# Retention outputs copied from their banks and normalised by ScalarE, row scaling on VectorE, background blocks loaded one call ahead

## The chip, the core and the metric

The kernel runs on one core of a Trainium2 chip. The core's engines are named here as the profile names them: PE (TensorE, matmuls; PEld is its weight load), DVE (VectorE), ACT (ScalarE), POOL (GpSimd) and SP (SyncE, which issues most DMAs). The metric is the device time of one execution in microseconds (us). Before the change the median of 3 runs is 3018.64 us (3012.9 to 3021.43).

## What is computed

The reference is a trunk of two layers on 1024 rows of width 1024, batch 1, all in float32. The mixer of layer 0 is a gated delta net, that of layer 1 a retention; each layer ends with a convolutional feed-forward, and each half of a layer with a layer norm. Scale, shift and gate vectors come from a conditioning vector by a product with `ada_w`, six vectors per layer.

```
e = silu(c @ cond_w + cond_b)
for i in range(2):
    mod = e @ ada_w[i] + ada_b[i]
    sh1, sc1, g1, sh2, sc2, g2 = split(mod, 6)
    y = mixers[i](x * (1 + sc1) + sh1)
    x = layer_norm(ALPHA * x + (1 + g1) * y, ln_g[i, 0], ln_b[i, 0])
    y = conv_ffn(x * (1 + sc2) + sh2, ...)
    x = layer_norm(ALPHA * x + (1 + g2) * y, ln_g[i, 1], ln_b[i, 1])
```

Retention has 4 heads (keys of 256, values of 512) and works in 8 chunks of 128 rows. A chunk's output is a masked score product plus the running state times the scaled queries; each row of it, 512 wide, is then standardised and gated:

```
o = intra + inter                       # per head and chunk: 128 x 512
o = (o - mean(o)) * rsqrt(var(o) + 1e-6)
o = o * silu(gate)
y = o @ w_out
```

## The kernel before

**Order of the work.** The stages follow each other: the delta net (to about 620 us in the profile), its output projection with layer norm, the first feed-forward (Strassen-like products `strassen`, then the down projection `proj_gen`), retention's projections (again `strassen`, 1440 to 1785), retention's chunks (1785 to 2180), its output projection, and the second feed-forward. Large products run as three float32r matmuls of a high and a low part; `split` (L88) makes the parts, the high one on ACT (L89), the low one on DVE (L90).

The kernel is written in a language whose scheduler puts instructions on the engines. It takes them in the order of the program, skips what isn't ready in its own time model, gives a tile a buffer of its tag (`BUFS`, L43: a tag and its number of buffers) when one is free, and sets the semaphores. On the chip each engine then runs its list in order, and so does each DMA queue. For the delta net and retention's chunks a planner of the kernel itself (`run`, L649) fixes the order on PE: generators yield a delay in planned microseconds, a matmul adds its price to the planned clock (`pm`, L637, 0.216 each), a transpose 0.109 (`ptr`), and the generator of the lowest priority number that is due goes next. What a generator yields after it hands work to the other engines is the time that the plan grants them; for retention these are in `RL` (L1799).

**Background work.** `bg` is a list of small units that don't belong to the stage in which they run. `bg_step` (L119) takes the first and runs it; it is called after a weight block in the delta net's filler, in `ret_v` (L1672), twice in each item `wino` of `strassen` (L1233, L1238), and in the projections. There are two kinds of unit.
- `bg_ada` (L201): a modulation vector, 8 units each. A unit loads a block of `ada_w`, 128 x 2 x 512 (`mvw`, L210), on SP, and DVE multiplies it by two values of `e` per row and adds (L214, L216). The tile's tag is `wr`, in `strassen` `lane` (`bg_tag`).
- `bg_gain` (L370): 16 units that multiply a block of 128 x 512 of the second-layer input by `ln_g` and add `ln_b` on POOL (L381, L382), and store it. The tile's tag is `lane`. Its only call is L1817, ahead of retention's chunks; its units run in the first 16 calls from `ret_v`.

**The tag `wr`.** It has two buffers of 4 KB per partition. They hold the raw weights of `load_w` (L100), both halves `wa` and `wb` of an item in `wino` (L1211), the blocks of `bg_ada`, some blocks in `proj_gen`, and at the start four transposed input blocks (`hold`, L532). `hold` puts two more into the tag `xT`, which nothing else uses.

**Retention's chunks.** `core(h)` (L1704) goes through the chunks of head h. Per chunk it makes the products of the keys with the values into two `sc` banks and the new state from them on DVE (L1728, L1730), calls `ret_front` (L1680) for the next chunk (scores and scaled keys, `kz` on ACT and DVE, `sThl`, and `qx` on POOL, L1701), and then the output `po` in an `sc` bank. There are two `sc` banks, and a chunk takes three in turn, so a bank in which `po` stands is wanted again by the next chunk's second key product. `ret_back` (L1748) works on the output: statistics from the bank on DVE (L1750, L1752), plus 1e-6 (L1753), to the power -0.5 on POOL (L1754, a 128 x 1 instruction), and the normalisation from the bank into `on` on DVE (L1756). It yields `RL["b"]`; then PE transposes `on` (L1763), DVE multiplies by the gate (L1765), and the blocks go to memory, some after sums on POOL (L1787). `on` shares the tag `t2` (3 buffers) with `kz`. Between the chunks, `ret_fill` (L1802) gives PE the value projections (`ret_v`) and the first two products of the output projection.

Of the kernel before, what the change touches and what calls it, by code (L numbers as in the profile page):

```python
# [12 lines left out]
ALU = mybir.AluOpType  # L13
AX = mybir.AxisListType

P = 128
# [17 lines left out]
def trunk_kernel(ctx: ExitStack, tc, A):  # L34
# [9 lines left out]
            "wr": 2, "wh": 2, "wl": 2, "t2": 3, "sm": 14, "sm2": 6, "st": 8, "s8": 6, "S": 4, "qx": 3, "fs": 1, "xT": 2}  # L44
# [74 lines left out]
    def bg_step(tile=mm_tile):  # L119
        bg_ps[0] = tile  # L120
        if bg:
            bg.pop(0)()
# [78 lines left out]
    def bg_ada(i, j, kind):  # L201
        box = {}

        def unit(nh, kp):
# [3 lines left out]
            wr = tl(bg_tag[0], [P, 2, HALF], name="mvw")  # L208
            c0 = j * D + nh * HALF
            sp.dma_start(wr, A["ada_w"][i, kp * 256:(kp + 1) * 256, c0:c0 + HALF].rearrange("(a p) n -> p a n", p=P))  # L210
# [30 lines left out]
        for nh in range(2):  # L241
            for kp in range(KT // 2):
                bg.append(lambda nh=nh, kp=kp: unit(nh, kp))
# [126 lines left out]
    def bg_gain(n, src, dst):  # L370
        gb = []

        def unit(c, r):
# [7 lines left out]
            pool.tensor_tensor(x, x, gb[0], ALU.mult)  # L381
            pool.tensor_tensor(x, x, gb[1], ALU.add)  # L382
# [149 lines left out]
    def hold(half, fs):  # L532
        for f in fs:
# [4 lines left out]
            else:  # L538
                t = tl("auh" if half else "xT", [P, HALF], name="xT")
# [614 lines left out]
    def strassen(hT0, xts, scale, shift, items, tags=("hTb", "hTb", "qkv", "qkv", "aux"), direct=False):  # L1154
        B = {"11": hT0[:4], "21": hT0[4:]}
# [592 lines left out]
    def ret_back(h, n, po):  # L1748
        st = tl("st", [P, 2, 6], name="rst")
        dve.bn_stats(st[:, 0], po)  # L1750
        mv = tl("s8", [P, 4], name="mv")
        dve.bn_aggr(mv[:, 0:2], st[:, 0])  # L1752
        dve.tensor_scalar(mv[:, 2:3], mv[:, 1:2], 1e-6, None, ALU.add)  # L1753
        pool.tensor_tensor(mv[:, 3:4], mv[:, 2:3], mhalf[:, 0:1], ALU.pow)  # L1754
        on = tl("t2", [P, HALF], name="on")
        dve.tensor_scalar(on, po, mv[:, 0:1], mv[:, 3:4], ALU.subtract, ALU.mult)  # L1756
# [42 lines left out]
    RL = {"v": 2.57, "q": 5.9, "f": 3.35, "p": 0.55, "c": 2.75, "b": 3.21, "o": 4.42}  # L1799
# [17 lines left out]
    bg_gain(1, xs[1], xg[0])  # L1817
# [106 lines left out]
```

## Time and profile before

| | us |
|---|---|
| median of 3 runs | 3018.64 |
| the profiled execution | 3028.18 |
| its span in the trace | 3026.4 |
| mean granted PE clock | 0.974 |
| PE, DVE, ACT, POOL busy | 2846.3, 2248.8, 1316.6, 672.8 |

How to read the profile's lines: a group or an instruction is given by its line in the kernel (L90 is a helper's, so the tile names tell what it works on), its engine, and out<-in by the tiles' names. A group's line ends with busy time, mean ns of one, and the idle time of its engine just before, with what ended it. In a list of waits, "A <- B: 7.5, 4, 4.1" says that A's engine stood idle for B, 7.5 us in 4 places, the longest 4.1. In a list by time the first number is the start in us, the second the duration, and brackets hold the idle time ahead and its releaser; SPq and ACTq are the queues from which DMAs are issued. In a list of an instruction's line, three numbers after the count are its shortest, median and longest ns. `sc`, `acc` and `mm` are PSUM banks.

### The profile page before, as it was taken

Reading aid. Unit: us, or ns where it says so; the run is one execution under the profiler, and the core shown is the slowest. Engines: PE = TensorE matmul, PEld = TensorE weight load, DVE = VectorE, ACT = ScalarE, POOL = GpSimd, SP = SyncE. Lnnn points to the kernel's source line nnn. Section 1 sums busy time; section 2 is a strip of 40 time slices with the busy share of each in tenths; the row PEclk is TensorE's granted clock in tenths of the full one; section 3 lists DMA queues with packets and bytes.
Section 4 is the critical chain, followed back from the end, with each engine's and each line's share of the span. In section 5 each row is a group of like instructions: output and inputs, shape, how many; then the busy total and the mean of one; then the engine's idle time right before and its main releaser. Section 6 shows DMA issues by size and latency. Waiting matters only on the chain.

```text
span 3026.4 us, 38855 instructions
## 1 busy us (share of the span) xinstructions
PE 2846.3 (94%) x13638; PEld 2316.4 (77%) x13638; DVE 2248.8 (74%) x3805; ACT 1316.6 (44%) x2409; POOL 672.8 (22%) x629
## 2 busy tenths in 40 slices
PE   8889998999999999998999999999998899999997
PEld 7768877887778888786777787767776688888785
DVE  5785786545778888998688645666788787778988
ACT  4655555434544444445433342221343544445442
POOL 0410311034011111630023302532200011113704
PEclk9999998999999999999999999999999999999998
DMA  7222222344344444864322444656663343335662
GB/s 274 87 70 74 97 82 64 116 163 137 105 153 156 154 153 158 322 201 154 129 91 101 173 155 143 212 175 181 210 224 123 108 139 105 105 104 202 250 196 108
DMA packets 243027, 450.22 MB, mean 149 GB/s; under 512 B 22928, under 2 KB 76432, under 8 KB 242832
## 3 DMA queue, kind: packets, MB, share of 16 engines
q1 hardware_dynamic: 211648, 400.02, 40.1%
q10 hardware_dynamic: 29760, 43.00, 3.9%
q0 software_dynamic: 1424, 4.72, 0.4%
q8 instruction: 107, 1.75, 0.2%
q14 instruction: 88, 0.72, 0.1%
HBM read 339.13 MB, written 108.53 MB: 148 GB/s over the span
## 4 chain that ended last, share of the span: by engine, by line
PE 34%; DVE 10%; DMA 6%; issue 3%; ACT 1%; POOL 1%; SPq 0%; POOLq 0%; DVEq 0%; ACTq 0%
PE acc L638 6%; PE acc L1160 5%; PE acc L110 3%; PE acc L111 3%; PE acc L112 3%; PE sc L1160 2%; PE sc L638 2%; PE acc L279 2%; PE acc L280 2%; PE acc L278 2%; DVE ab L90 1%; PE sc L110 1%; PE sc L112 1%; PE sc L111 1%; DVE bb L90 1%
## 5 line engine op out<-in xcount | busy, mean ns | idle before, releaser
L638 PE MATMUL acc<-hT,wh 128*128 128x512 f32 x960 | 304.4, 399 | 0.0
L1558 POOL TENSOR_TENSOR o<-o 128x512 f32<-128x512 f32 x88 | 118.8, 1360 | 726.7 <-DVE o L1551 653.5
L1160 PE MATMUL acc<-T,wb 128*128 128x512 f32 x840 | 208.8, 399 | 14.6 <-DVE wb L90 14.6
L279 PE MATMUL acc<-bb,ab 128*128 128x512 f32 x504 | 203.3, 403 | 18.6 <-DVE bb L90 18.5
L638 PEld LDWEIGHTS acc<-hT,wh 128*128 128x128 f32 x960 | 185.5, 193 | 34.9
L278 PE MATMUL acc<-bb,ab 128*128 128x512 f32 x504 | 191.7, 404 | 20.2 <-DVE ab L90 11.5
L638 PE MATMUL acc<-hT,wl 128*128 128x512 f32 x480 | 205.7, 429 | 0.2 <-ACT sg L1086 0.2
L1160 PEld LDWEIGHTS acc<-T,wb 128*128 128x128 f32 x840 | 160.3, 192 | 53.1 <-DVE wb L90 19.7
L280 PE MATMUL acc<-bb,ab 128*128 128x512 f32 x504 | 200.7, 399 | 0.0
L89 ACT ACTIVATE ab<-ar 128x512 fp32r<-128x512 f32 x210 | 129.7, 624 | 163.1 <-PE acc L280 84.0
L90 DVE TENSOR_TENSOR wb<-wr,wb 128x512 fp32r<-128x512 f32 x162 | 116.1, 719 | 102.3 <-ACT wb L89 102.3
L90 DVE TENSOR_TENSOR ab<-ar,ab 128x512 fp32r<-128x512 f32 x210 | 177.0, 850 | 13.8 <-ACT ab L89 13.5
L90 DVE TENSOR_TENSOR wl<-wr,wh 128x1024 fp32r<-128x1024 f32 x85 | 107.3, 1262 | 96.8 <-ACT wh L89 96.8
L90 DVE TENSOR_TENSOR wb<-mm,wb 128x512 fp32r<-128x512 f32 x216 | 144.7, 683 | 20.8 <-ACT wb L89 18.8
L89 ACT ACTIVATE wh<-wr 128x1024 fp32r<-128x1024 f32 x101 | 106.8, 1059 | 120.5 <-PE acc L638 48.3
L1217 ACT ACTIVATE pc<-acc 128x512 f32<-128x512 f32 x143 | 84.7, 593 | 166.2 <-PE acc L1160 95.3
L89 ACT ACTIVATE wb<-mm 128x512 fp32r<-128x512 f32 x216 | 122.3, 593 | 67.1 <-DVE mm L1206 66.2
L89 ACT ACTIVATE wb<-wr 128x512 fp32r<-128x512 f32 x162 | 98.6, 626 | 97.8 <-DMA wr<-in_ffn_up 50.7
L638 PE MATMUL acc<-wh,hT 128*128 128x512 f32 x384 | 136.5, 418 | 1.6 <-DVE vv L90 1.6
L457 DVE SCALAR_TENSOR_TENSOR qkv<-raw,vc,qkv 128x512 f32<-128x512 f32 x144 | 114.6, 800 | 30.4 <-ACT qkv L455 29.2
L1537 DVE SCALAR_TENSOR_TENSOR o<-g,vc,o 128x512 f32<-128x512 f32 (+2 forms) x176 | 134.7, 783 | 1.2 <-ACT o L1532 0.5
L278 PEld LDWEIGHTS acc<-bb,ab 128*128 128x128 f32 x504 | 96.1, 193 | 47.9 <-DVE ab L90 13.1
(634 smaller groups left out, 7774.6 us busy)
## 6 DMA issues: line engine op xcount, KB each, us to landing
wr<-in_ffn_up SPq DMA_DIRECT2D x96, 512.0 KB, 4.1
mvw<-in_ada_w SPq DMA_DIRECT2D x80, 512.0 KB, 4.3
ad<-o SPq DMA_DIRECT2D x154, 256.0 KB, 2.6
ar<-ad SPq DMA_DIRECT2D x154, 256.0 KB, 4.7
Br<-in_ffn_down SPq DMA_DIRECT2D x88, 256.0 KB, 3.7
wr<-in_ret_wv SPq DMA_DIRECT2D x32, 512.0 KB, 3.7
ar<-od SPq DMA_DIRECT2D x56, 256.0 KB, 5.4
xs<-xt ACTq DMA_DIRECT2D x24, 512.0 KB, 3.4
```

The costliest lines, as they stand in the source:

```text
L89: act.activation(dst_h, src, AF.Copy)
L90: eng.tensor_tensor(dst_l, src, dst_h, ALU.subtract)
L110: mm(acc, wl[:, k], hl[0], start=first, stop=False)
L111: mm(acc, wh[:, k], hl[1], start=False, stop=False)
L112: mm(acc, wh[:, k], hl[0], start=False, stop=last)
L278: mm(acc, a[1][:, sl], w[0], start=first, stop=False)
L279: mm(acc, a[0][:, sl], w[1], start=False, stop=False)
L280: mm(acc, a[0][:, sl], w[0], start=False, stop=last)
L638: pq(pe.matmul(out, lhsT, rhs, start=start, stop=stop), cost)
L1160: return pe.matmul(*a, skip_group_check=True, **kw)
L1537: dve.scalar_tensor_tensor(tv, gv[:, c0 - j:c1 - j], w[:, 2 - j:3 - j], tv, ALU.mult, ALU.add)
L1558: pool.tensor_tensor(o[d], o[x], o[y], op)
```

## The change

1. `bg_step` issues the load of the next unit, where that has one that can go ahead (`fetch`), before it runs the current unit. A unit is now a pair of its fetch and its work. `bg_flush` runs a unit whose load is out already, at the start and at the end of `strassen`, so that no loaded tile crosses the change of tag.
2. `wr` has 3 buffers instead of 2. The tag `xT` is gone; its two tiles are `cv` tiles now.
3. `bg_gain` takes its tiles from `wr`, and its multiplication and addition run on the engine given, DVE for its only call. The first block of each column half has no fetch ahead.
4. `ret_back`: ACT copies `po` from the bank to `on`; the statistics are taken from `on`; the factor and the shift (minus mean times factor) are made by small instructions, two on DVE and two on POOL; ACT normalises `on` in place with them. `RL["b"]` is 6.0 instead of 3.21.

```diff
-            "wr": 2, "wh": 2, "wl": 2, "t2": 3, ..., "fs": 1, "xT": 2}
+            "wr": 3, "wh": 2, "wl": 2, "t2": 3, ..., "fs": 1}
...
-    def bg_step(tile=mm_tile):
+    def bg_step(tile=mm_tile, ahead=True):
         bg_ps[0] = tile
         if bg:
-            bg.pop(0)()
+            unit = bg.pop(0)[1]
+            if ahead and bg and bg[0][0]:
+                bg[0][0]()
+                bg_ahead[0] = True
+            else:
+                bg_ahead[0] = False
+            unit()
+
+    bg_ahead = [False]
+
+    def bg_flush():
+        if bg_ahead[0]:
+            bg_step(ahead=False)
...
     def bg_ada(i, j, kind):
         box = {}
+        def fetch(nh, kp):
+            wr = box[nh, kp] = tl(bg_tag[0], [P, 2, HALF], name="mvw")
+            c0 = j * D + nh * HALF
+            sp.dma_start(wr, A["ada_w"][i, kp * 256:(kp + 1) * 256, c0:c0 + HALF].rearrange("(a p) n -> p a n", p=P))
+
         def unit(nh, kp):
...
-            wr = tl(bg_tag[0], [P, 2, HALF], name="mvw")
-            c0 = j * D + nh * HALF
-            sp.dma_start(wr, A["ada_w"][i, kp * 256:(kp + 1) * 256, c0:c0 + HALF].rearrange("(a p) n -> p a n", p=P))
+            if (nh, kp) not in box:
+                fetch(nh, kp)
+            wr = box.pop((nh, kp))
...
-                bg.append(lambda nh=nh, kp=kp: unit(nh, kp))
+                bg.append((lambda nh=nh, kp=kp: fetch(nh, kp), lambda nh=nh, kp=kp: unit(nh, kp)))
...
-    def bg_gain(n, src, dst):
-        gb = []
-
-        def unit(c, r):
+    def bg_gain(n, src, dst, eng=pool):
+        gb, box = [], {}
+
+        def fetch(c, r):
             if r == 0:
                 gb[:] = [tl("auh", [P, HALF], name="gb") for _ in range(2)]
                 for t, nm in zip(gb, ("ln_g", "ln_b")):
                     sp.dma_start(t, A[nm][n:n + 1, hs(c)].to_broadcast([P, HALF]))
-            x = tl("lane", [P, HALF], name="xg")
-            rs = slice(r * P, r * P + P)
-            sp.dma_start(x, src[rs, hs(c)])
-            pool.tensor_tensor(x, x, gb[0], ALU.mult)
-            pool.tensor_tensor(x, x, gb[1], ALU.add)
-            sp.dma_start(dst[rs, hs(c)], x)
+            x = box[c, r] = tl("wr", [P, HALF], name="xg")
+            sp.dma_start(x, src[r * P:r * P + P, hs(c)])
+
+        def unit(c, r):
+            if (c, r) not in box:
+                fetch(c, r)
+            x = box.pop((c, r))
+            eng.tensor_tensor(x, x, gb[0], ALU.mult)
+            eng.tensor_tensor(x, x, gb[1], ALU.add)
+            sp.dma_start(dst[r * P:r * P + P, hs(c)], x)
...
-                bg.append(lambda c=c, r=r: unit(c, r))
+                bg.append((r and (lambda c=c, r=r: fetch(c, r)), lambda c=c, r=r: unit(c, r)))
...
-                t = tl("auh" if half else "xT", [P, HALF], name="xT")
+                t = tl("auh", [P, HALF], name="xT") if half else tl("cv", [P, 516], name="xT")[:, 0:HALF]
...
     def strassen(hT0, xts, scale, shift, items, tags=("hTb", "hTb", "qkv", "qkv", "aux"), direct=False):
+        bg_flush()
...
+        bg_flush()
         bg_tag[0] = "wr"
         return B
...
     def ret_back(h, n, po):
         st = tl("st", [P, 2, 6], name="rst")
-        dve.bn_stats(st[:, 0], po)
+        on = tl("t2", [P, HALF], name="on")
+        act.activation(on, po, AF.Copy)
+        dve.bn_stats(st[:, 0], on)
         mv = tl("s8", [P, 4], name="mv")
         dve.bn_aggr(mv[:, 0:2], st[:, 0])
-        dve.tensor_scalar(mv[:, 2:3], mv[:, 1:2], 1e-6, None, ALU.add)
-        pool.tensor_tensor(mv[:, 3:4], mv[:, 2:3], mhalf[:, 0:1], ALU.pow)
-        on = tl("t2", [P, HALF], name="on")
-        dve.tensor_scalar(on, po, mv[:, 0:1], mv[:, 3:4], ALU.subtract, ALU.mult)
+        dve.tensor_scalar(mv[:, 1:2], mv[:, 1:2], 1e-6, None, ALU.add)
+        dve.tensor_scalar(mv[:, 2:3], mv[:, 0:1], -1.0, None, ALU.mult)
+        pool.tensor_tensor(mv[:, 3:4], mv[:, 1:2], mhalf[:, 0:1], ALU.pow)
+        pool.tensor_tensor(mv[:, 2:3], mv[:, 2:3], mv[:, 3:4], ALU.mult)
+        act.activation(on, on, AF.Identity, bias=mv[:, 2:3], scale=mv[:, 3:4])
         yield RL["b"]
...
-    RL = {"v": 2.57, "q": 5.9, "f": 3.35, "p": 0.55, "c": 2.75, "b": 3.21, "o": 4.42}
+    RL = {"v": 2.57, "q": 5.9, "f": 3.35, "p": 0.55, "c": 2.75, "b": 6.0, "o": 4.42}
...
-    bg_gain(1, xs[1], xg[0])
+    bg_gain(1, xs[1], xg[0], dve)
```

More of the change, by code (lines that the diff above doesn't have):

```diff
@@ L43, in trunk_kernel @@
     BUFS = {"hTa": 8, "hTb": 8, "qkv": 24, "aux": 4, "auh": 8, "lane": 4, "cv": 4, "ada": 1,
-            "wr": 2, "wh": 2, "wl": 2, "t2": 3, "sm": 14, "sm2": 6, "st": 8, "s8": 6, "S": 4, "qx": 3, "fs": 1, "xT": 2}
+            "wr": 3, "wh": 2, "wl": 2, "t2": 3, "sm": 14, "sm2": 6, "st": 8, "s8": 6, "S": 4, "qx": 3, "fs": 1}
     def tl(tag, shape, dt=F32, name=None):
```

## The prediction

> **What bounds the kernel now.** I read the page first (span and engines), then the busy times by stage, then who waits for whom on PE within two stages, then the instructions in order of time around the longest of those waits.
>
> ```profile
> span 3026.4 us, 38855 instructions
> PE 2846.3 (94%) x13638; PEld 2316.4 (77%) x13638; DVE 2248.8 (74%) x3805; ACT 1316.6 (44%) x2409; POOL 672.8 (22%) x629
> ```
>
> PE is busy 94% of the span, so all waits of PE together are worth 3026.4 - 2846.3 = 180 us. The change takes no matmul away. What it can win is part of these 180 us and the slow clock that follows idle time. The stages that the change reaches (stretch, its length, busy us and instructions of PE, weight load, DVE, ACT and POOL, then PE's clock, DMA share, GB/s):
>
> ```profile
> 0.00:620.00 620.00, 559.60 (x3648) 475.69 (x3649) 425.33 (x1016) 328.06 (x698) 105.74 (x169) 0.95 0.32 108
> 1440.00:1690.00 250.00, 238.90 (x1052) 193.81 (x1052) 193.36 (x269) 85.34 (x143) 58.64 (x39) 1.00 0.32 111
> 1785.00:2180.00 395.00, 372.24 (x1660) 287.95 (x1659) 242.98 (x430) 100.65 (x169) 123.96 (x168) 0.99 0.60 186
> 2180.00:2355.00 175.00, 158.59 (x678) 125.94 (x678) 139.57 (x232) 74.20 (x125) 10.58 (x13) 0.95 0.51 176
> 2355.00:2775.00 420.00, 411.15 (x1791) 336.61 (x1790) 319.05 (x483) 200.20 (x339) 55.58 (x41) 0.99 0.34 112
> ```
>
> In order: the delta net (60 us of idle PE), retention's Strassen projections (11), retention's chunks (23), retention's output projection (16), the second feed-forward's Strassen products (9). In the chunk stage PE waits for these:
>
>
> ```profile
> PE sc L638 <- DVE on L1756: 7.5, 4, 4.1
> PE mm L641 <- DVE on L1756: 5.1, 3, 2.5
> ```
>
> The first row is a matmul that wants the `sc` bank still held by a chunk's output, the second the transposes of that output; together 12.6 of the 23 us. The longest one, in order of time:
>
> ```profile
> 1869.37 0.70 DVE L1750 BATCH_NORM_STATS2 rst<-sc 128x6 f32<-128x512 f32 x1 [0.75 <-PE sc L638]
> 1870.96 1.29 POOL L381 TENSOR_TENSOR xg<-xg,gb 128x512 f32<-128x512 f32 x1 [8.78 <-DMA xg<-xs]
> 1872.21 1.84 POOL L1701 TENSOR_TENSOR qx<-qk,dx 128x128 f32<-128x128 f32 x2
> 1874.02 1.25 POOL L382 TENSOR_TENSOR xg<-xg,gb 128x512 f32<-128x512 f32 x1
> 1876.06 0.54 POOL L1754 TENSOR_TENSOR mv<-mv,mhalf 128x1 f32<-128x1 f32 x1
> 1876.63 0.81 DVE L1756 TENSOR_SCALAR on<-sc,mv 128x512 f32<-128x512 f32 x1 [3.31 <-POOL mv L1754]
> 1877.50 1.65 PE L638 MATMUL sc<-vv,kz 128*128 128x512 f32 x3 [4.05 <-DVE on L1756]
> ```
>
> The statistics were ready soon after 1870.1, but the tiny power instruction stood on POOL behind the row gains (L381, L382, loaded late) and `qx`, and the bank was freed only by L1756, 8 us after bn_stats began. Without that queue 0.70 + 0.18 + 0.15 + 0.54 + 0.81, about 2.4 us, would do.
>
> **The change part by part.** Prices of single instructions:
>
> ```profile
> L1756 DVE TENSOR_SCALAR on<-sc,mv 128x512 f32<-128x512 f32 x32 | 25.9, 809 | 32.0 <-POOL mv L1754 32.0
> L1752 DVE BATCH_NORM_AGGREGATE mv<-rst 128x2 f32<-128x6 f32 x32 | 5.7, 178 | 0.7
> L1753 DVE TENSOR_SCALAR mv<-mv 128x1 f32<-128x1 f32 x32 | 4.9, 154 | 1.1
> L1754 POOL TENSOR_TENSOR mv<-mv,mhalf 128x1 f32<-128x1 f32 x32 | 17.9, 561 | 83.6 <-DVE mv L1753 83.6
> L381 POOL TENSOR_TENSOR xg<-xg,gb 128x512 f32<-128x512 f32 x16 | 22.4, 1404 | 86.7 <-issue 49.5 <-DMA xg<-xs 37.2
> L90 DVE TENSOR_TENSOR wb<-wr,wb 128x512 fp32r<-128x512 f32 x162 | 116.1, 719 | 102.3 <-ACT wb L89 102.3
> L1217 ACT ACTIVATE pc<-sc x73: 574/597/602, 853.5 to 2786.9; 128x512 f32<-128x512 f32 x73
> L1374 ACT ACTIVATE xt<-xt,mv x8: 799/814/819, 2966.8 to 3020.0; 128x512 f32<-128x512 f32 x8
> ```
>
> *Loads of the engines.* DVE loses 32 x 0.809 = 25.9 and gains 32 x 0.154 = 4.9 for the sign and 32 x 0.719 = 23.0 for the gains: +2 us on 243 busy of 395 (a gain has two inputs in SBUF like the subtraction that it is priced as; that took 1.44 beside POOL in the row of 1573.33 below, which would make it +25). POOL loses 32 gains at 1.40 (44.9; L382 is priced as L381) and gets 32 multiplications, not shown and priced as the power at 0.561 (18.0): -27. ACT gets 32 x (0.597 + 0.814) = +45 on 101 of 395. None becomes full.
>
> *(a) Bank and chain.* The `sc` bank is freed by the copy, 0.6 us after the last matmul instead of 2.4 to 8. That takes the 7.5 us row away unless ACT is late. The output's own chain grows: 0.60 copy, 0.70 statistics (on SBUF now, priced as from the bank), 0.18, two times 0.15, two times 0.56, 0.81: 3.7 us against 2.4. The planner however places the transposes 6.00 instead of 3.21 after the last matmul. Slack goes from 0.8 to 2.3 us, and the gains leave POOL's queue. Of the 5.1 us of late transposes I expect half to stay. Sum 7.5 + 2.5 = **10 won**, between 0 and 12.6. Queued behind the waiting ACT instruction are `kz`, `sThl` and the weight splits; ACT idles before most `kz` (row in the rivals), which is their cover.
>
> *(b) Background loads one call ahead.* The same DMAs on SP, each issued one call earlier. In the chunk stage two waits of DVE for a modulation block stop PE:
>
> ```profile
> 2007.91 1.90 DVE L216 SCALAR_TENSOR_TENSOR ada<-mvw,e,ada 128x512 f32<-128x512 f32 x2 [6.43 <-DMA mvw<-in_ada_w]
> 2011.54 0.50 PE L638 MATMUL acc<-wl,22_12882 128*128 128x512 f32 x1 [2.20 <-DVE wl L90]
> 2016.60 0.75 DVE L216 SCALAR_TENSOR_TENSOR ada<-mvw,e,ada 128x512 f32<-128x512 f32 x1 [3.86 <-DMA mvw<-in_ada_w]
> 2019.80 0.96 PE L638 MATMUL sc<-vv,sThl 128*128 128x512 f32 x3 [2.76 <-DVE Sr L1728]
> ```
>
> 10.3 us of DVE's wait cost PE 5.0, about half. Loaded a call earlier both vanish: **4.5 won**, between 0 and 5. Against that, the first gain block of each column half isn't fetched ahead and now stops DVE, not POOL. POOL's waits for such loads were 37.2 us over 16 blocks (row of L381), 2.3 each; two of them, of which PE sees half: **2 lost**, between 0 and the 8.8 of the longest (row of 1870.96). A load that is called for earlier also stands earlier in SP's queue, and when its buffer isn't free, the gate loads, weights and stores behind it wait:
>
> ```profile
> L210 SPq EVENT_SEMAPHORE  x55: 17/28/8337, 59.2 to 2453.2; - x55
> ```
>
> SP has waited up to 8.3 us there, 0.03 in the median; I price it at nothing, because the third buffer is added at the same time. In the delta net:
>
> ```profile
> DVE ada L216 <- DMA mvw<-in_ada_w: 11.8, 10, 2.1
> PE mm L638 <- DVE DT L955: 19.8, 2, 11.0
> ```
>
> There DVE runs the triangular solve without a break up to the two long PE waits, so a microsecond of its waits is one of PE's. Only some of the ten lie in those stretches: **3 won**, between 0 and 11.8.
>
> *(c) Third `wr` buffer.* In the rotary items of the Strassen projections both halves of an item's weights are requested only after the last use of the previous ones:
>
> ```profile
> PE acc L1160 <- DVE wb L90: 4.7, 4, 1.7
> PE sc L1160 <- DVE wb L90: 3.2, 3, 1.3
> 1568.40 0.33 SPq L1212 DMA_DIRECT2D wr<-in_ret_wqk  x1
> 1571.82 0.69 DVE L1151 TENSOR_TENSOR pc<-sc,pc 128x512 f32<-128x512 f32 x1 [2.14 <-PE sc L1160]
> 1572.67 1.16 ACT L89 ACTIVATE wb<-wr 128x512 fp32r<-128x512 f32 x2 [3.02 <-DMA wr<-in_ret_wqk]
> 1573.33 2.88 DVE L90 TENSOR_TENSOR wb<-wr,wb 128x512 fp32r<-128x512 f32 x2 [0.82 <-ACT wb L89]
> ```
>
> ACT waits 3.02 us for the load and DVE stands idle 2.14 + 0.82 there; some 13 us later DVE is behind and PE waits up to 1.7. With a third buffer the first block is in before, and the 2.9 us of splits move into that idle time. Of 7.9 us I take **6 won**, between -3 (a new order of DVE's work) and 7.9. What the third buffer does in the feed-forward stages I leave at nothing: their loads lie beside matmuls that keep PE busy 411 of 420 us, and if the new order of DVE's work uncovers them, it costs the same 3. The freed `xT` tag costs nothing either, since its two tiles go into `cv` buffers that nothing else uses yet. The flushes around the Strassen call only run units that would run anyway.
>
> *(d) Clock.* After idle time the clock falls; three such slices lie in the chunk stage, of which the first and the last:
>
> ```profile
> 1877.30:1880.70 3.40, 3.20 (x12) 2.91 (x13) 1.43 (x3) 0.24 (x1) 0.00 (x0) 0.50 0.80 256
> 2020.70:2024.10 3.40, 3.40 (x10) 2.63 (x9) 2.08 (x7) 0.31 (x1) 1.39 (x3) 0.50 0.57 218
> ```
>
> Each costs half of 3.4 us. If the waits ahead of them go, 5.1 us go with them: **3 won**, between 0 and 5.1. The Trainium skill, "TensorE: Matmul & The Clock Gate", section "What's actually happening", has the clock halved only after an idle window of about 3.4 us; by that only the 4.05 us wait counts, term (d) is 1.7 and the sum about 1 us less. The trace disagrees, with 0.50 after a wait of 2.76 too.
>
> *(e) End of the stage.* The last output is ready later by the chain's 1.3 us or, where the planner rules, by 2.8; the output projection behind it already idles 16 us: **2 lost**, between 0 and 2.8.
>
> Sum: 10 + 4.5 - 2 + 3 + 6 + 3 - 2 = 22.5 us less. The profiled execution took 3028.2 us (span 3026.4), 9.5 above the median of 3018.64. It goes to about 3005.7, and with the same difference a median of **2996**.
>
> **Rivals.**
>
> *The wide one:* all the waits named go and the ends of the terms hold: 12.6 + 5 + 11.8 + 7.9 + 5.1 - 2 = 40 us less, 2978. Speaks for it that the rows name exact culprits, against it that PE's order stays written by hand.
>
> *It does less than it says:* the scheduler already issued loads as soon as a buffer was free, and `wr` now holds gains and modulation blocks besides weights, so a block "one call ahead" can still wait for its buffer. Then (b) and (c) give nothing, and (a) counts with the two losses: 10 - 2 - 2 = 6 less, 3013.
>
> *Slower: the longer chain is what PE waits for.* One mechanism, at the transposes L1763. Work of 3.7 us meets a plan of 6.0, so it decides when queueing on DVE, POOL and ACT exceeds 2.3 us in the usual chunk. In the row of 1876.63 it was 5.7 (8.1 elapsed less 2.4), though mostly behind gains that leave POOL. If each of 32 chunks is late by the 1.3 us that the chain grew, that is 42; less the bank's 7.5, the 5.5 net of (b) and the 6 of (c), 23 more: 3042. Against it speaks ACT's room:
>
> ```profile
> ACT kz L1692 <- PE mm L641: 84.6, 27, 9.3
> ```
>
> ACT idles 3.1 us before a `kz` on average, more than the 1.4 that it gets per chunk. The Trainium skill, "ScalarE: Activation LUTs", section "Rules for kernel authors", sends additions and multiplications to VectorE, not ScalarE, and so speaks for this rival; the trace has both passes at 0.81, so only the copy is extra.
>
> **How the numbers follow.** Forecast 0.55, the wide one 0.12, doing less 0.19, slower 0.14. A measurement of this kernel can tell about 0.3% (9 us) from no change, so faster means under 3009.6. All of the first two and a quarter of the third give faster 0.72; the rest of the third and a little of the fourth same 0.16; slower 0.12. The forecast alone spans 2986 to 3008. The range runs from the wide case, 2978, past doing less to 3020, and leaves out most of the slower case and the tail below the wide one, under 0.2.
>
> **What would show it.** Right: no row of PE waiting for the `sc` bank on the normalisation; POOL's wait ahead of the power shorter; no DVE wait over 2 us for `mvw` after the first block; ACT's wait for `in_ret_wqk` near nothing and PE's `wb` rows gone. Wrong: PE waits at L1763's transposes over 10 us, DVE waits for `xg`, or SP holds weights behind a block that has no buffer.

## The result, and the profile after

The median after the change is 3033.3 us of 11 runs (3024.1 to 3039.19), beside 3021.46 us of 11 runs of the kernel before on the same chip. The ratio is 1.0027, with a 95% interval of 1.0015 to 1.0039: the change costs about 8 us. Forecast were 22.5 us less. The profiled execution of the kernel after took 3035.15 us. Line numbers move: L638 is now L659, L641 L662, L1160 L1182, L278 L295, L279 L296, L381 L402, L216 L233, and the output's path is L1774 (copy) to L1782 (normalisation).

The head of the page of the kernel after:

```profile
span 3033.3 us, 39038 instructions
PE 2859.4 (94%) x13638; PEld 2312.7 (76%) x13638; DVE 2256.3 (74%) x3837; ACT 1358.1 (45%) x2473; POOL 640.5 (21%) x629
```

The engines got about what the prediction gave them (DVE +7.5 us for +2, ACT +41.5 for +45, POOL -32 for -27). What it has nothing for is PE: the same 13638 matmuls keep it busy 13.1 us longer (2859.4 against 2846.3). That isn't a wait, so no list of waits shows it. Two stretches of 280 us in the second feed-forward, in which PE never stands still, show it best; first the kernel before, then the kernel after (columns as in the stage rows of the prediction):

```profile
2480.00:2760.00 280.00, 280.00 (x1235) 231.53 (x1234) 206.74 (x311) 130.41 (x222) 44.55 (x32) 1.00 0.32 108
```

```profile
2480.00:2760.00 280.00, 280.00 (x1222) 228.97 (x1221) 206.16 (x306) 128.55 (x218) 44.59 (x32) 1.00 0.30 104
```

PE is busy for all of the 280 us at full clock in both, but gets 1235 matmuls done before and 1222 after: 226.7 against 229.1 ns each. The matmuls themselves became slower.

PE's waits in the chunk stage of the kernel after (1773 to 2180):

```profile
PE acc L659 <- DVE vv L90: 12.2, 7, 3.8
PE sc L659 <- DVE Sr L1753: 4.6, 3, 4.0
PE acc L659 <- DVE ab L90: 3.4, 1, 3.4
PE mm L662 <- ACT on L1782: 2.5, 2, 1.4
```

The 7.5 us for the `sc` bank are gone, and the transposes' 5.1 have become 2.5, as forecast. In their place PE waits 12.2 us for the low parts of the values (`vv`) and 4.6 for the state `Sr`; the same two in the kernel before (L1730 is now L1753):

```profile
PE acc L638 <- DVE vv L90: 1.6, 2, 1.0
PE sc L638 <- DVE Sr L1730: 0.7, 1, 0.7
```

PE's waits for `wb` in retention's projections were 8.0 and 3.2 us before (1440 to 1785) and are now, from 1430 to 1773:

```profile
PE acc L1182 <- DVE wb L90: 2.1, 5, 0.5
PE sc L1182 <- DVE wb L90: 1.1, 3, 0.4
```

To place the gains and losses I take the start of PE's n-th matmul in each profiled execution, since PE's list has 13638 in all kernels of this study that compute the reference. The time in us between chosen matmuls:

| stage | matmuls | before | after |
|---|---|---|---|
| delta net, its output projection begun | 0 to 3750 | 633.0 | 633.9 |
| first feed-forward | 3750 to 6450 | 639.1 | 636.0 |
| its down projection | 6450 to 7050 | 144.3 | 140.7 |
| retention's projections | 7050 to 8550 | 362.6 | 356.3 |
| retention's chunks | 8550 to 10200 | 393.1 | 403.7 |
| its output projection | 10200 to 10950 | 191.2 | 194.5 |
| second feed-forward | 10950 to 12700 | 411.6 | 414.6 |
| last down projection | 12700 to 13600 | 222.2 | 224.4 |

The change wins 12 us up to retention's chunks, loses 11 in these and 8.5 behind them. Each column is one execution, so a small difference in one stage says little: the kernel e3 below runs the same instructions as the kernel before, and its stages differ from it by up to 1.4; the last down projection, at which no experiment is aimed, takes 221.4 to 229.9 us in those that keep the old layout.

### The profile page after: what moved, and what is told of

Its sections match the earlier page's. It is cut to its first block, busy times and chain, and to the rows that moved or that the text cites. A ratio compares the mean times of both kernels' runs of the same rounds, so it can differ in the third digit from the quotient of the medians.

```text
span 3033.3 us, 39038 instructions
## 1 busy us (share of the span) xinstructions
PE 2859.4 (94%) x13638; PEld 2312.7 (76%) x13638; DVE 2256.3 (74%) x3837; ACT 1358.1 (45%) x2473; POOL 640.5 (21%) x629
## 4 chain that ended last, share of the span: by engine, by line
PE 69%; DVE 12%; DMA 9%; ACT 4%; issue 4%; POOL 1%; SPq 0%; POOLq 0%; DVEq 0%; ACTq 0%
PE acc L659 15%; PE acc L1182 9%; PE acc L110 5%; PE acc L111 5%; PE acc L112 5%; PE sc L1182 4%; PE sc L659 4%; PE acc L295 3%; PE acc L296 3%; PE acc L297 3%; PE mm L659 2%; PE sc L110 2%; PE sc L111 2%; PE sc L112 2%; DMA mvw<-in_ada_w 1%
## 5 line engine op out<-in xcount | busy, mean ns | idle before, releaser
L659 PE MATMUL acc<-hT,wh 128*128 128x512 f32 x960 | 302.5, 397 | 0.0
L296 PE MATMUL acc<-bb,ab 128*128 128x512 f32 x504 | 205.0, 407 | 11.7 <-DVE bb L90 11.4
L1182 PE MATMUL acc<-T,wb 128*128 128x512 f32 x840 | 207.8, 396 | 5.8 <-DVE wb L90 5.8
L659 PEld LDWEIGHTS acc<-hT,wh 128*128 128x128 f32 x960 | 184.2, 192 | 34.7
L295 PE MATMUL acc<-bb,ab 128*128 128x512 f32 x504 | 192.9, 408 | 16.3 <-DVE xt L1381 8.3
L659 PE MATMUL acc<-hT,wl 128*128 128x512 f32 x480 | 204.3, 426 | 0.3 <-ACT sg L1107 0.3
L1182 PEld LDWEIGHTS acc<-T,wb 128*128 128x128 f32 x840 | 158.1, 189 | 44.4 <-DVE wb L90 8.8
L90 DVE TENSOR_TENSOR ab<-ar,ab 128x512 fp32r<-128x512 f32 x210 | 165.4, 794 | 19.9 <-ACT ab L89 19.8
L659 PE MATMUL acc<-wh,hT 128*128 128x512 f32 x384 | 137.3, 417 | 12.2 <-DVE vv L90 12.2
L1560 DVE SCALAR_TENSOR_TENSOR o<-g,vc,o 128x512 f32<-128x512 f32 (+2 forms) x176 | 143.1, 828 | 5.4 <-ACT o L1555 4.7
L89 ACT ACTIVATE bb<-Bw 128x512 fp32r<-128x512 f32 x120 | 74.5, 625 | 124.9 <-PE acc L297 55.8
```

The costliest lines, as they stand in the source:

```text
L89: act.activation(dst_h, src, AF.Copy)
L90: eng.tensor_tensor(dst_l, src, dst_h, ALU.subtract)
L295: mm(acc, a[1][:, sl], w[0], start=first, stop=False)
L296: mm(acc, a[0][:, sl], w[1], start=False, stop=False)
L659: pq(pe.matmul(out, lhsT, rhs, start=start, stop=stop), cost)
L1182: return pe.matmul(*a, skip_group_check=True, **kw)
```

## The experiments

All ratios are to the kernel before, run on the same chip; 0.0010 is 3.0 us.

**Where the slower matmuls come from.** Nothing in the change touches the feed-forwards' matmuls but their place in memory. SBUF is full, a tag's buffers are laid out at its first use, and `hold` now uses `cv` ahead of `aux`, `wr`, `qkv` and `auh`. `cv` has four buffers of 2080 bytes, so these four tags moved from 544 bytes above a multiple of 2048 to 672. `hTa`, `hTb`, `wh` and `wl` stayed at 544.

*e1_before_moved: that part alone.*

```diff
-            "wr": 2, ..., "fs": 1, "xT": 2}
+            "wr": 2, ..., "fs": 1}
...
-                t = tl("auh" if half else "xT", [P, HALF], name="xT")
+                t = tl("auh", [P, HALF], name="xT") if half else tl("cv", [P, 516], name="xT")[:, 0:HALF]
```

> The kernel before with one part of the change alone: the two tiles of the tag xT become cv tiles, wr keeps its two buffers. Every engine's list of instructions stays the same, in the same order; only addresses move: cv is now laid out ahead of aux, wr, qkv and auh, and its four buffers of 2080 bytes put those at 672 bytes above a multiple of 2048 where they lay at 544. hTa, hTb, wh and wl stay at 544. Theory: a matmul that streams from an aux or qkv tile is slower at the new addresses while its weights lie at the old ones; in the dense stretches of the changed kernel the spacing of the 128x512 matmuls adds 21 us more to the shortest one than in the kernel before, so about 3021 + 21 = 3042. Rival (the addresses do nothing, the time went to the new order of the work): within 3 us of the kernel before, 3018 to 3024.

Measured: 1.0038 (1.0024 to 1.0051), 11.5 us slower, with the same instructions in the same order on every engine. The same stretch as above has

```profile
2480.00:2760.00 280.00, 280.00 (x1219) 228.45 (x1218) 204.17 (x310) 126.21 (x214) 38.94 (x28) 1.00 0.31 104
```

229.7 ns per matmul, so the addresses alone do it. Half of the expected 21 us arrives. Against e3 (below; the same instructions, all addresses moved alike) the second feed-forward, where PE is the bound, takes 3.7 us more (415.1 against 411.4 for matmuls 10950 to 12700), the first 3.1, the chunks 3.9, the two down projections together 0.5. In the down projections PE waits for DVE in between; that the slower matmuls take from those waits is the likely reason for the missing half, and isn't shown. The chunks' 3.9 are mostly the granted clock, which stood at 0.50 for 20.5 us of them in e1 and for 13.7 in e3; half of that difference is 3.4.

*e2_after_aligned: the whole change in the old layout.*

```diff
-                t = tl("auh", [P, HALF], name="xT") if half else tl("cv", [P, 516], name="xT")[:, 0:HALF]
+                t = tl("auh" if half else "qkv", [P, HALF], name="xT")
```

> The changed kernel with the two tiles that hold took from cv taken from qkv, so that cv is laid out late again and every tile of aux, wr, qkv and auh stands at 544 bytes above a multiple of 2048. Instructions and their order are those of the changed kernel but for two loads on SP at the start. Theory: the 21 us of slower matmuls go, 3033 - 21 = 3012, about 9 us faster than the kernel before, and what is left is the change's own worth (the prediction had 22.5). Rival (addresses do nothing): 3033, within 3 us.

Measured: 0.9969 (0.9957 to 0.9982), so without the moved addresses the change wins 9.4 us. To the kernel after that is 17.6 us (1.0027 - 0.9969 = 0.0058), more than e1's 11.5; the intervals of about 4 us on each allow both, and I take 11 to 18.

*e3_before_shift: all addresses moved by 128.*

```diff
-    sb = ctx.enter_context(tc.tile_pool(name="sb", bufs=1))
+    cp.tile([P, 32], F32, tag="pad", name="pad"); sb = ctx.enter_context(tc.tile_pool(name="sb", bufs=1))
...
-                t = tl("auh" if half else "xT", [P, HALF], name="xT")
+                t = tl("auh" if half else "qkv", [P, HALF], name="xT")
```

> The kernel before with all tiles moved by the same 128 bytes (a pad in front; hold's two tiles from qkv to make room), so that weights and streamed operands all stand at 672 above a multiple of 2048. It tells two forms of the theory apart. If the place of the streamed operand alone decides, every 128x512 matmul is slower and the time rises by more than the 21 us, to 3042 or over. If the distance between the weights and the streamed operand decides, it stays at 3021, within 3 us. Rival (addresses do nothing): 3021 too.

Measured: 0.9999 (0.9987 to 1.001). Moving all of it alike does not matter, so what is left is the distance between a matmul's weights and its streamed operand.

*e4_addr_matmuls: that distance by itself.* The core of the kernel:

```python
    for w, m in PAIRS:
        acc = [ps.tile([P, HALF], F32, tag="acc", name=f"w{w}m{m}", bufs=8) for _ in range(4)]
        for k in range(8):
            h = [(M0 + m + j * 2048 + (k % 4) * 4096) // 4 for j in range(2)]
            for n in range(4):
                c = (W0 + w + n * 1024 + (k % 2) * 512) // 4
                for i, (wo, hi) in enumerate(((c + 1024, h[0]), (c, h[1]), (c, h[0]))):
                    pe.matmul(acc[n], big[:, wo:wo + P], big[:, hi:hi + HALF], start=k == 0 and i == 0,
                              stop=k == 7 and i == 2)
```

> A kernel that leaves all of the reference's work out: 20 groups of 96 float32r matmuls 128x512 with the order of mm3, weights and streamed operand in one tile at chosen bytes above a multiple of 2048 (the PSUM tile's name tells them: w544m672 has weights at 544, the streamed operand at 672). No other engine works beside them but for the copies out of PSUM. If the streamed operand's place decides: w544m544 and w672m544 at 227 ns per matmul, w544m672 and w672m672 at about 233. If the distance decides: w672m672 at 227, w544m672 and w672m544 at 233. If it takes the traffic of other engines as well: all at 227.

Measured: each row is a window from the first matmul of a group of 96 to the first of the next group. In order: weights and streamed operand at (544, 672), (672, 672), (672, 544), (544, 608), (544, 640), (544, 800), (544, 548).

```profile
34.91:57.24 22.33, 22.33 (x97) 18.02 (x96) 4.46 (x7) 0.00 (x0) 0.00 (x0) 1.00 0.00 0
57.24:79.02 21.78, 21.78 (x97) 18.02 (x96) 2.71 (x5) 0.00 (x0) 0.00 (x0) 1.00 0.00 1
79.02:101.41 22.39, 22.39 (x97) 18.02 (x96) 2.82 (x5) 0.00 (x0) 0.00 (x0) 1.00 0.00 1
123.81:145.78 21.97, 21.97 (x97) 18.03 (x96) 2.72 (x5) 0.00 (x0) 0.00 (x0) 1.00 0.00 0
145.78:168.20 22.42, 22.42 (x98) 18.02 (x97) 2.82 (x5) 0.00 (x0) 0.00 (x0) 1.00 0.00 1
235.46:257.22 21.76, 21.76 (x97) 18.02 (x96) 2.70 (x5) 0.00 (x0) 0.00 (x0) 1.00 0.00 1
411.98:434.82 22.84, 22.84 (x98) 18.22 (x96) 2.83 (x5) 0.00 (x0) 0.00 (x0) 1.00 0.00 1
```

Divided by 96: 232.6 ns at a distance of 128 bytes, 226.9 at 0 (both at 672), 233.2 at -128, 228.9 at 64, 233.5 at 96, 226.7 at 256, 237.9 at 4. DVE does no more than copy the four banks of each group out, and the DMA share is 0.00, so it is PE's own two operands. The pairs (0, 0), (512, 512) and (544, 1056) gave 226.7 to 226.9 too. The distance decides, and 0, 256 and 512 are equally good. The Trainium skill, "SBUF — State Buffer", section "SBUF: two separate sides", says that PE never waits on anyone there; between two engines nothing here speaks against it, but PE's own weights and stream cost each other up to 5%.

**What the parts are worth in the old layout.** The next runs all start from e2 or the kernel before, with weights and streams at a distance of a multiple of 256. First one part is taken away at a time.

*e5_gains_pool: gains back on POOL.*

```diff
-    bg_gain(1, xs[1], xg[0], dve)
+    bg_gain(1, xs[1], xg[0], pool)
```

> The changed kernel in the layout of e2 (weights and streamed operands at the same bytes above a multiple of 2048; 0.9969 of the kernel before), with the row gains back on POOL, still in wr tiles and fetched a call ahead. In e2 DVE waits 31.2 us in 14 places for the gain's blocks, and PE then 12.4 us for DVE's vv and 5.8 for Sr. Theory (gains on DVE cost what the chunk stage lost): 8 us less than e2, a ratio of about 0.994 to the kernel before. Rival (POOL's queue of gains, qx and the power makes the normalisation late again, and PE waits for on at the transposes instead): within 3 us of e2, 0.996 to 0.998, with the transposes' wait at 5 us or more.

*e6_no_retback: the normalisation of the kernel before.* `ret_back` and `"b": 3.21` as in the lines with a minus in the diff of the change.

> The layout and all parts of e2, but the output's normalisation as before the change: statistics and normalisation from the bank on DVE, the plan's 3.21. The prediction's term (a) says 10 us are lost by that: a ratio to the kernel before of 1.000 against e2's 0.997, with 7 us or more of PE waits for the sc bank on L1756's instruction. With the gains also on DVE it can be more, 1.002. Rival (what the bank's early release wins is lost at once to other waits on DVE): within 3 us of e2, 0.996 to 0.998.

*e7_wr2: two buffers.*

```diff
-            "wr": 3, "wh": 2,
+            "wr": 2, "wh": 2,
```

> The layout and all parts of e2, with two wr buffers instead of three. By the traces e2 gains 9 us on a kernel of the old parts in the rotary items and some 9 in the first feed-forward. Theory (the third buffer does both): 12 to 18 us more than e2, 1.001 to 1.003 of the kernel before. The prediction's term (c) alone: 6 us more, 0.999. Rival (the loads ahead do it, not the buffer): within 3 us of e2.

*e8_no_ahead: nothing fetched ahead.*

```diff
-            if ahead and bg and bg[0][0]:
+            if False and ahead and bg and bg[0][0]:
```

> The layout and all parts of e2, with no background block fetched ahead. The prediction's (b) has 4.5 us in the chunk stage and 3 in the delta net won by it: 7.5 us more than e2, 0.9995 of the kernel before; with the gains on DVE each of their loads would be waited for in full, 14 places by 2 us more: up to 1.003. Rival (the scheduler issues a load as soon as a buffer is free, so the program's order does not matter): within 3 us of e2, 0.996 to 0.998.

Measured: e5 0.9962 (0.9949 to 0.9975), e6 0.9962 (0.9947 to 0.9977), e7 1.0061 (1.0037 to 1.0085), e8 1.0007 (0.9992 to 1.0022). So taking either retention part away loses nothing: both rivals hold, and the theory of e5 falls as far as it goes by the engine. The intervals leave some 6 us either way, so the 10 us of term (a) are excluded in e6, and a few us are not. e7 is worse than any theory had it: with two buffers the change costs 18 us (28 against e2). The likely reason is that a block that lies ready, or a gain's tile, holds one of the two buffers that the weights need. ACT in e7's chunk stage (1785 to 2200):

```profile
ACT wh L89 <- DMA wr<-in_ret_wv: 57.2, 13, 8.1
```

13 waits for a value projection's weights, where e2 has four. e8 shows that the loads ahead are worth 11.5 us beside three buffers, more than the 7.5 forecast; where they lie is told under (b).

In e6 PE waits in the chunk stage (1770 to 2200) for

```profile
PE sc L659 <- DVE on L1779: 8.9, 6, 2.6
PE mm L662 <- DVE on L1779: 5.3, 5, 2.3
PE acc L659 <- DVE vv L90: 4.2, 2, 3.5
```

14.2 us of waits for the normalisation are back, where e2 has 2.5, and 8.2 of e2's 12.4 for `vv` and 5.5 of its 5.8 for `Sr` are gone: the change has exchanged one for the other.

*e9_loads_only: both retention parts undone* (the edits of e5 and e6 together).

> What is left of the change when both retention parts are undone in the layout of e2: the third wr buffer and the loads one call ahead, with the normalisation of the kernel before (L1756's) and the gains on POOL. e2 is at 0.9969 of the kernel before, e5 and e6 each 0.0007 lower. Theory (the two retention parts each move a wait and win nothing): 0.9955, no slower than e2. Rival (they hold each other up: gains on POOL stand ahead of the power again, and the bank's 7.5 and the transposes' 5.1 us of before come back on top): 0.999 to 1.000.

*e10_wr3_only: the kernel before with the third buffer alone.*

```diff
-            "wr": 2, "wh": 2, ..., "fs": 1, "xT": 2}
+            "wr": 3, "wh": 2, ..., "fs": 1}
...
-                t = tl("auh" if half else "xT", [P, HALF], name="xT")
+                t = tl("auh" if half else "qkv", [P, HALF], name="xT")
```

> The kernel before with a third wr buffer alone (hold's two tiles from qkv make the room; all addresses as in e2). The prediction's (c) gives it 6 us: 0.998. From e7, where the loads ahead without the third buffer cost 18 us, and e8, where all but the loads ahead is at 1.0007: the buffer is worth little by itself and the loads ahead are worth little by themselves, 0.999 to 1.001, and only both together win 10 or more. Rival (the buffer is the whole gain): 0.995 to 0.9965.

*e11_copy_dve_pool and e12_copy_dve_dve: copy on ACT, normalisation on DVE from the copy;* gains on POOL in e11, on DVE in e12; the small instructions are those of the kernel before.

```diff
-        act.activation(on, on, AF.Identity, bias=mv[:, 2:3], scale=mv[:, 3:4])
+        dve.tensor_scalar(on, on, mv[:, 0:1], mv[:, 3:4], ALU.subtract, ALU.mult)
...
-    RL = {..., "b": 6.0, "o": 4.42}
+    RL = {..., "b": 4.0, "o": 4.42}
```

> e5 (gains on POOL) with the output still copied from its bank by ACT, but normalised from the copy on DVE, and the plan's time for it 4.0 instead of 6.0. In e5 ACT stands 67.9 us for POOL's factor with the splits of the weights behind it, DVE then 50.5 us for wh, and PE 10.3 us for vv and 5.6 for on. Theory (ACT's wait in its own queue is what eats the early release of the bank): the waits for vv fall by half or more, no wait for the sc bank on the normalisation, 5 to 8 us less than e5: 0.9935 to 0.9945. Rival (DVE, back at 26 us more work in the stage, is late instead): 0.996 to 0.998.

> e11 with the gains on DVE as in the changed kernel. If DVE's waits for the gain blocks (31.2 us in e2, 33.7 in e6) are hidden behind ACT's late splits in e2, they show here: 3 us or more slower than e11. If they cost PE nothing: the same as e11 within 2 us.

Measured: e9 0.9958 (0.9942 to 0.9974), e10 0.9975 (0.9959 to 0.9991), e11 0.996 (0.9945 to 0.9975), e12 0.9977 (0.9967 to 0.9987). e9: the retention parts win nothing, together either. e10 lies between its theory and its rival: 7.6 us, near the 6 of the prediction's (c). e11's theory falls: the waits for `vv` are 7.3 us there, but PE now waits 14.1 for the transposes:

```profile
PE mm L662 <- DVE on L1780: 14.1, 8, 3.0
PE acc L659 <- DVE vv L90: 7.3, 4, 3.5
```

e12 is 5 us slower than e11, which is what the theory of loads that show on a busy DVE asks for, though the intervals meet.

The table of stages now had an odd row. Retention's chunks (matmuls 8550 to 10200) took 400.4 to 406.0 us in e2, e5, e6, e8, e9, e11 and e12, 387.8 in e10. Common to the slow ones is none of the retention parts and, with e8 among them, not the loads ahead: it is that the gains' tiles come from `wr`. (e7, with two `wr` buffers, took 415.2.)

*e13 to e16: gains' tiles from `lane` again, not fetched ahead.* e13 is e9 with this edit, e14 is e5 with it, e15 e11, e16 e2.

```diff
-            x = box[c, r] = tl("wr", [P, HALF], name="xg")
+            x = box[c, r] = tl("lane", [P, HALF], name="xg")
...
-                bg.append((r and (lambda c=c, r=r: fetch(c, r)), lambda c=c, r=r: unit(c, r)))
+                bg.append((None, lambda c=c, r=r: unit(c, r)))
```

> e9 with the gains as in the kernel before (lane tiles, not fetched ahead, POOL), so that only modulation blocks are loaded ahead and wr serves the weights of the value projections alone in the chunk stage. Theory (the gain tiles keep wr buffers from the weights and move the stage's loads and splits): the stage falls from 401 us to 388 or so, the whole to 0.9958 - 0.0035 = 0.992. Rival (the modulation blocks loaded ahead do it): 0.996, stage at 400.

> e13 with the changed normalisation (copy and normalisation on ACT, plan 6.0). The prediction's (a): 10 us less than e13, and no waits for the sc bank. Rival from e2, e5 and e6 (ACT's wait for POOL's factor holds the splits, PE waits for vv and kz in place of the bank): the same as e13 within 3 us.

> e13 with the output copied from its bank by ACT and normalised from the copy on DVE, plan 4.0. If the bank's early release is worth something once ACT doesn't wait for POOL: 5 us less than e13. If the copy only makes the transposes later (in e11 PE waited 14.1 us for them): the same or up to 5 us more.

> All of the change in the layout of e2, but the gains' tiles from lane and not fetched ahead; they stay on DVE. If the tiles' tag decides: 10 us less than e2, 0.9935. If the engine decides (DVE stops for each block): as e2 or slower, 0.997 to 0.999.

Measured, with the stage in the profiled execution:

| | ratio | interval | chunks, us |
|---|---|---|---|
| e13: loads ahead, normalisation as before | 0.9946 | 0.9926 to 0.9965 | 394.3 |
| e14: and copy and normalisation on ACT | 0.9945 | 0.9925 to 0.9965 | 393.3 |
| e15: and copy on ACT, normalisation on DVE | 0.9965 | 0.9951 to 0.9978 | 402.9 |
| e16: as e14, gains on DVE | 0.9938 | 0.9919 to 0.9957 | 392.8 |

The tag decides, not the engine: e16 is 9.4 us below e2 by the edit, of which the stage shows 10.0, and e14, with the gains on POOL, takes the same as e16 within the intervals. It isn't the granted clock, which stood at 0.50 for 17.1 us of the stage in both e2 and e16. The same edit wins less elsewhere: 3.6 us from e9 to e13 and 5.1 from e5 to e14 (7.0 and 7.6 in the stage), and nothing from e11 to e15, where PE waits 16.9 us for the transposes. e15 comes near its second expectation, with 5.8 us more than e13, but its profiled execution was the slowest of its 12, so its 402.9 may be too long. e13 itself falls halfway between its theory (388 and 0.992) and its rival (400 and 0.996): more of this under (b). DVE's and ACT's waits for loads in e2's chunk stage, and below it DVE's in e16's:

```profile
DVE xg L402 <- DMA xg<-xs: 31.2, 14, 5.9
ACT wh L89 <- DMA wr<-in_ret_wv: 12.9, 4, 7.3
```

```profile
DVE xg L402 <- DMA xg<-xs: 9.5, 6, 2.9
```

With `lane` tiles that aren't called for ahead DVE waits 9.5 us for the blocks, not 31.2: three `wr` buffers shared by gains, modulation blocks and weights bring each block later than four `lane` buffers do without any fetch. In e8, with `wr` tiles and no fetch, DVE waits 30.6 us for them, so the fetch isn't what delays them. ACT doesn't wait for `in_ret_wv` at all in e16's chunk stage. e14 against e13 is the output's path by itself: nothing, where 10 us less were forecast; the two intervals leave some 8 us either way. e16 beats both kernels, 18.8 us below the kernel before.

## Why the prediction was wrong, point by point

**"The freed `xT` tag costs nothing either, since its two tiles go into `cv` buffers that nothing else uses yet."** This is the step that turned the sign. It looked at who uses the buffers, and not at what their earlier first use does to the layout. The prediction put it at nothing; it costs 11 to 18 us (e1, and e2 against the kernel after). Without it the change wins 9.4 us (e2), which is still less than half of the 22.5; the points below are about the rest of the miss.

**(a) 10 won for bank and chain: 0** (e6 against e2, e14 against e13). The waits named did go. But the cover named for the waiting ACT, its idle time before `kz`, was the wrong one: what stands behind a late normalisation in ACT's list are the splits of `vv` and of the weights, and the list below shows them start only after it. The instructions in order of time around one of the seven waits for `vv`, in the kernel after:

```profile
1988.95 0.75 DVE L233 SCALAR_TENSOR_TENSOR ada<-mvw,e,ada 128x512 f32<-128x512 f32 x1 [0.80 <-DMA mvw<-in_ada_w]
1989.69 0.14 DVE L1779 TENSOR_SCALAR mv<-mv 128x1 f32<-128x1 f32 x1
1990.55 0.60 POOL L1781 TENSOR_TENSOR mv<-mv 128x1 f32<-128x1 f32 x1
1991.18 0.82 ACT L1782 ACTIVATE on<-on,mv 128x512 f32<-128x512 f32 x1 [4.04 <-POOL mv L1781]
1991.90 1.06 ACT L89 ACTIVATE vv<-acc 128x512 fp32r<-128x512 f32 x2
1992.51 1.29 DVE L90 TENSOR_TENSOR vv<-acc,vv 128x512 fp32r<-128x512 f32 x2 [1.42 <-ACT vv L89]
1993.25 0.50 PE L659 MATMUL acc<-wh,hT 128*128 128x512 f32 x1 [1.78 <-DVE vv L90]
```

DVE stands for a modulation block, the small instructions behind it are late, then POOL's factor, ACT has stood 4.04 us for it, and only then come the high part of `vv` on ACT, the low part on DVE, and PE, which has waited 1.78 us for the bank of the value projection. All in all ACT's waits there are, in the kernel after,

```profile
ACT on L1782 <- POOL mv L1781: 52.6, 20, 4.0
```

and PE's waits for `vv` in the chunk stage of e13, with the normalisation as before, and below it of e14, with both passes on ACT:

```profile
PE acc L659 <- DVE vv L90: 1.0, 1, 1.0
```

```profile
PE acc L659 <- DVE vv L90: 7.4, 5, 2.4
```

The same step from e9 to e5 takes them from 1.0 to 10.3. The long chain that the slower rival feared is there, but PE pays for it mostly at the value projections and little at the transposes (2.5 us in the kernel after), and about as much as the bank's release wins. That this exchange comes out even within the 6 to 8 us of the intervals is shown (e6, e14); why it is even, and not somewhat more or less, is only argued.

**(b) Background loads ahead, 4.5 in the chunks, 2 lost by the gains, 3 in the delta net: the delta net's size was about right, the other two failed.** The stages in us, of one execution each (e10: third buffer alone; e8: all but the loads ahead; e2 and e13: with both):

| stage | before | e10 | e13 | e8 | e2 |
|---|---|---|---|---|---|
| delta net | 633.0 | 638.9 | 634.1 | 639.7 | 635.5 |
| first feed-forward | 639.1 | 639.0 | 628.7 | 637.0 | 629.3 |
| retention's chunks | 393.1 | 387.8 | 394.3 | 402.3 | 402.8 |

The gains' 2 us were 9.4 (e16 against e2), and not for the first block of a half: DVE waited for 14 of 16 blocks. The tag was the shortage, not the time of the request. In the chunk stage nothing of the 4.5 is seen. From e8 to e2 DVE's waits for modulation blocks fall from 16.9 to 5.1 us as forecast, and the stage takes the same. From e10 to e13 it takes 6.5 us more, of which the granted clock is about 5 (at 0.50 for 10.2 us in e10, 20.5 in e13). In the delta net the loads ahead win 4 to 5 us (e10 to e13, e8 to e2), but the third buffer, for which the prediction had nothing there, first loses 6. DVE's waits for the blocks fell from 11.8 us in the kernel before to the first row in the kernel after; PE's waits for the solve, the second row, did not:

```profile
DVE ada L233 <- DMA mvw<-in_ada_w: 3.7, 4, 1.3
PE mm L659 <- DVE DT L976: 26.1, 2, 14.6
```

They rose from 19.8 to 26.1, and to 28.1 in e10, which has the buffer and no load ahead, and to 26.5 in e7, which has the loads ahead and no third buffer. The end of a solve (the transpose `RX<-T`) in the kernel before, then after:

```profile
470.24 1.25 DVE L813 STREAM_TRANSPOSE RX<-T 128x1024 f32<-128x1024 f32 x1
```

```profile
477.95 1.25 DVE L834 STREAM_TRANSPOSE RX<-T 128x1024 f32<-128x1024 f32 x1
```

From the last weight split ahead of it to that transpose it is 16.7 us before and 21.1 after. In DVE's list two modulation products (L214, L216) stand in between before, six (L231, L233) after, four more at 0.75 us. The scheduler has put six there in e7, e8 and e10 too: blocks that can come earlier are used earlier, and here that is inside the steps that PE waits for.

What the loads ahead won most by lies where the prediction had nothing: the first feed-forward, 629 to 632 us in the eleven kernels of the old layout that load ahead. The same stretch before and in e13:

```profile
755.00:1240.00 485.00, 471.27 (x2061) 381.52 (x2060) 394.55 (x613) 235.46 (x446) 73.00 (x58) 0.99 0.49 161
```

```profile
755.00:1240.00 485.00, 475.03 (x2099) 388.63 (x2098) 411.36 (x622) 238.56 (x449) 89.11 (x66) 0.99 0.50 166
```

38 matmuls more in 485 us, at 0.227 each 8.6 us. PE's idle time fell by 3.8 us only (13.7 to 10.0), so more than half of the gain lies inside what counts as busy: the busy share of 471 in 485 had hidden it. What paces PE there, and which wait the loads ahead removed, isn't settled.

**(c) Third buffer in the rotary items, 6 won: right for that stage**, which wins 6.0 us by it in e10 (362.6 to 356.6). That e10 as a whole wins a similar 7.6 is partly luck: by the table above the chunks win 5 there and the delta net loses 6, and the prediction had neither.

**(d) Clock, 3 won: the other way.** The chunk stage of the kernel after, and the slices of it at half the clock:

```profile
1773.00:2180.00 407.00, 381.05 (x1659) 289.75 (x1658) 235.76 (x462) 140.06 (x235) 104.27 (x181) 0.97 0.59 187
1815.00:1821.80 6.80, 6.00 (x14) 4.74 (x15) 4.28 (x7) 0.00 (x0) 0.00 (x0) 0.50 0.46 157
1856.00:1862.80 6.80, 6.16 (x13) 3.61 (x14) 4.51 (x9) 1.17 (x3) 0.00 (x0) 0.50 0.84 265
1999.40:2002.80 3.40, 3.40 (x9) 2.61 (x9) 0.00 (x0) 0.00 (x0) 0.85 (x2) 0.50 1.04 325
2122.20:2129.00 6.80, 6.04 (x14) 4.80 (x15) 2.39 (x6) 2.48 (x4) 1.88 (x4) 0.50 1.07 381
```

The granted clock is 0.97 there, 0.99 before. It stood at 0.50 for 23.8 us, not for the 10.2 of the three slices before; by the term's own price, half of that time, some 7 us are lost in place of the 3 won. The waits ahead of the old slices went, but the first two of the new ones begin in the waits of 3.8 us for `vv` and 4.0 for `Sr`, which came in their place. In e2 it is 17.1 us, and 13.7 in e3, whose instructions are those of the kernel before, so a few us of this differ from one execution to the next.

**(e) End of the stage, 2 lost: about right.** It is 3.3 by the table (191.2 to 194.5), just beyond the range given, and 0.5 to 2.5 where only the normalisation differs (e6 to e2, e9 to e5, e13 to e14); all of that is close to what the stage differs by itself.

Together, with the measured values: (a), with what it does to (d) and (e), 0; (c) 7.6; the loads ahead 8.8 (e10 to e13); the gains' tag -9.4. That makes about 7 won where e2 measures 9.4, and the layout takes 11 to 18. Of the signs of being wrong that the prediction named, DVE's wait for `xg` showed, with 31.6 us in the kernel after, and the wait at the transposes did not.

Of the rivals, "does less than it says" with its 6 us came nearest to the 9.4 that the change wins in the old layout, but that is luck in the main: it had (c) and the loads ahead at nothing and (a) in full, and the runs show the reverse. What it had right is that `wr` is wanted by too many. The slower rival had the sign of the result, not its reason: its 23 us were to be lost at the transposes. None of the rivals had the layout.

## What to carry to other kernels

A change of tags or buffers is a change of addresses, so before matmuls are priced as unchanged, the places of their weights and streamed operands are to be compared; a count of matmuls over a stretch in which PE never stands still shows a slower pace that no list of waits does. A wait that is taken from one engine's list and given to another's has to be followed through everything that stands behind it there. And a load can be asked for earlier only if the tag has a buffer for it: count the buffers that are wanted at once before the request is moved.

## What the runs showed of the hardware

Float32r matmuls of 128x512 back to back take 226.7 to 226.9 ns when weights and streamed operand start 0, 256 or 512 bytes apart, 228.9 at 64, 232.6 to 233.5 at 96, 128 and -128, and 237.9 at 4 bytes (e4). Moving both alike by 128 bytes changes nothing (e3). The small instructions on POOL differ: in the trace after, the power (L1780) took 0.55 us in the median, the multiplication of the same 128x1 (L1781) 195 ns, where the prediction priced both at 561.
